# Two buffers for the tile of decays in the state-space part of a hybrid block, with decayed x and the states sharing one buffer and scaled x lying in the room of B

## The chip, the core and the metric

The kernel runs on one core of one Trainium2 chip. The metric is the device time of one launch in microseconds (us). The runs of the kernel before gave a median of 2721.82 us (2720.56, 2721.82 and 2723.49).

## What is computed

One layer of a residual block: an input projection of 512 tokens with 2048 channels, two branches (retention and a state-space scan, SSD), a projection of each back to 2048 channels, a gated merge and an output projection. The change touches the SSD scan alone. Cut to what matters (`xc` is x times its step size dt, `ac` the log decays of a chunk):

```python
def step(state, inp):
    xc, bc, cc, ac = inp
    acum = jnp.cumsum(ac, axis=1)
    seg = acum[:, :, None] - acum[:, None, :]
    decay = jnp.exp(jnp.where(causal, seg, -jnp.inf))
    cb = jnp.einsum('blgn,bsgn->blsg', cc, bc)
    y = jnp.einsum('blsg,blsgh,bsghp->blghp', cb, decay, xc)
    y = y + jnp.einsum('blgn,bghpn->blghp', cc, state) * jnp.exp(acum)[..., None]
    tail = jnp.exp(acum[:, -1:] - acum)
    state = (state * jnp.exp(acum[:, -1])[..., None, None]
             + jnp.einsum('bsgn,bsgh,bsghp->bghpn', bc, tail, xc))
    return state, y
```

There are 8 groups, each with its own B and C and with 8 heads of 64 channels; the kernel works in chunks of 128 tokens.

## The kernel before

All big projections go through `unit` (line 270). One unit multiplies 256 columns of a weight matrix with the normalized input, which stays in SBUF as a pair of fp32r tiles. Weights come in four loads (`wf`, line 244, on SP's queue); VectorE forms sums and differences of 128x128 blocks (lines 247, 252, 253), ScalarE rounds them to fp32r (`whi`, line 148), VectorE takes the remainder (`wlo`, line 149), and TensorE runs three matmuls of 256 columns for each of 7 blocks and 8 depths k (lines 230 to 232): 168 "block products" in a unit. `whi` has 7 buffers and `wlo` 6.

The SSD part (lines 593 to 709) lies between about 800 and 2010 us. For each group `g` one unit gives B and C; a convolution and SiLU (`conv`, lines 608 to 615) put them into `Bt` and `Ct`. `Bt` is transposed into `Bk` (lines 630 and 631), and `CB` is the masked product of `Bt` and `Ct` (lines 635 and 636); after line 635 nothing reads `Bt` until the next group writes it. Then, twice in a group (`jj`), a unit for x and a unit for z follow, and for each of the two halves `e` of the x unit a tile step:

- line 652 loads `E` on SP's queue; line 656 transposes x on TensorE; line 658 (VectorE) scales it into `xd`; line 661 (GpSimd, POOL) multiplies it by the decay to the end of its chunk into `xl`.
- line 665 (TensorE) forms the states from `xl` and `Bk`; lines 668 (ScalarE) and 672 (VectorE) carry them from chunk to chunk in `S`; line 693 (TensorE) multiplies them with `Ct`.
- line 678 loads `L`, two rows of cumulated log decays spread to 128 partitions, 512 KB, on SP's queue. Eight ScalarE instructions (line 682) and an exponential (line 684) make decays of it, VectorE multiplies by `CB` (line 685), and line 689 (TensorE) multiplies them with `xd`.
- lines 695 to 698 (VectorE) put the tile of y together, ScalarE squares and scales it, and it is stored.

So there are 32 tile steps: 8 groups, two pairs each, two halves in a pair. After each pair a gate unit is run (`gates`). `xd`, `xl`, `S`, `L` and `E` each have one buffer. Between the parts of a tile step stand block products of the next units, which the tile framework's scheduler sets there: it orders each engine's instructions by a model of their times and by priorities, and an engine then runs its instructions strictly in that order. Each of SP's loads waits in its queue for its buffer to come free, and what is queued behind it waits too.

The lines that the change touches are 657, 660, 667 and 677; in the changed kernel every line from 658 on has a number one higher.

Of the kernel before, what the change touches and what calls it, by code (L numbers as in the profile page):

```python
# [8 lines left out]
F32 = mybir.dt.float32  # L9
# [7 lines left out]
P = 128  # L17
T = 512
TB = T // P
# [108 lines left out]
def hybrid_block(tc, A, out):  # L128
# [15 lines left out]
    def att_tile():  # L144
        return att.tile([P, T], F32, name="att")
# [185 lines left out]
    def room(tag):  # L331
        return bg.tile([P, 8, 256], F32, name=tag, tag=tag)
# [170 lines left out]
    with tc.tile_pool(name="ret", bufs=1) as rp:  # L503
# [3 lines left out]
        for h in range(NH):  # L507
# [3 lines left out]
            c = h * DK  # L511
# [81 lines left out]
    with tc.tile_pool(name="ssd", bufs=1) as sp:  # L593

        cw = sp.tile([P, 48, 5], F32, name="cw")
        SP.dma_start(out=cw, in_=A["conv"])
        dsk = sp.tile([P, 32], F32, name="dsk")
        SP.dma_start(out=dsk, in_=A["dskip"])
        sq = R1
        sn = sp.tile([P, 32], F32, name="sn")  # L600
        SP.dma_start(out=sn, in_=A["ssd_norm_w"])
        g8 = room("A8").rearrange("p (n h) t -> p n (h t)", n=4)
        x8 = room("B8").rearrange("p (n h) t -> p n (h t)", n=4)
        Bt, Ct = g8[:, 0], g8[:, 1]
        Bk, CB = (g8[:, i].rearrange("p (c n) -> p c n", c=TB) for i in (2, 3))
        xs, sz = (x8[:, 0], x8[:, 1]), (x8[:, 2], x8[:, 3])

        def conv(x, j, dst):

            ACT.activation(dst, x, AF.Identity, scale=cw[:, j, 3:4], bias=cw[:, j, 4:5])  # L610
            for i in (2, 1, 0):
                s = 3 - i
                DVE.scalar_tensor_tensor(dst[:, s:], x[:, :T - s], cw[:, j, i:i + 1], dst[:, s:],
                                         op0=ALU.mult, op1=ALU.add)
            ACT.activation(dst, dst, AF.Silu)

        def gates(off, dst, i):
            w = w_in[:, off + i * 256:off + (i + 1) * 256]
            for e, x in enumerate(unit([w], plain=(2 * i + (off == GSO)) in PLAIN_M)):
                ACT.activation(x, x, AF.Sigmoid)  # L620
                ACT.dma_start(out=dst[(2 * i + e) * P:(2 * i + e + 1) * P, :], in_=x)

        todo = [(o, d, i) for i in range(NG) for o, d in ((GRO, gr_d), (GSO, gs_d))]
        for g in range(NG):
            xb, xc = unit([w_in[:, o + g * P:o + (g + 1) * P] for o in (BO, CO)], plain=g in PLAIN_B)
            conv(xb, 32 + g, Bt)
            conv(xc, 40 + g, Ct)
            ps = att_tile()
            for c in range(TB):
                PE.transpose(ps[:, c * P:(c + 1) * P], Bt[:, c * P:(c + 1) * P], ident)  # L630
            ACT.copy(Bk.rearrange("p c n -> p (c n)"), ps)
            ps = att_tile()
            for c in range(TB):
                sl = slice(c * P, (c + 1) * P)
                PE.matmul(ps[:, sl], Bt[:, sl], Ct[:, sl], start=True, stop=True)
            DVE.tensor_tensor(CB, ps.rearrange("p (c l) -> p c l", c=TB),
                              tri[:, None, :].to_broadcast([P, TB, P]), op=ALU.mult)

            for jj in range(2):
                j0 = g * 4 + jj * 2  # L640
                for e, x in enumerate(unit([w_in[:, XO + j0 * P:XO + (j0 + 2) * P]], plain=jj in PLAIN_X)):
                    conv(x, j0 + e, xs[e])
                for e, x in enumerate(unit([w_in[:, ZO + j0 * P:ZO + (j0 + 2) * P]], plain=jj in PLAIN_Z)):
                    ACT.activation(sz[e], x, AF.Silu)
                for e in range(2):
                    j = j0 + e
                    h0 = 2 * j
                    hs = slice(h0, h0 + 2)
                    y = xs[e]
                    E = sp.tile([P, T - P], F32, name="E")  # L650
                    for i in range(2):
                        SP.dma_start(out=E[i * 64:(i + 1) * 64, :], in_=E_d[h0 + i, P:].partition_broadcast(64))

                    ps = att_tile()
                    for c in range(TB):
                        PE.transpose(ps[:, c * P:(c + 1) * P], y[:, c * P:(c + 1) * P], ident)
                    xd = sp.tile([P, TB, 2, 64], F32, name="xd")
                    DVE.tensor_tensor(xd, ps.rearrange("p (c i d) -> p c i d", c=TB, i=2),  # L658
                                      dt[:, :, hs, None].to_broadcast([P, TB, 2, 64]), op=ALU.mult)
                    xl = sp.tile([P, TB - 1, 2, 64], F32, name="xl")  # L660
                    POOL.tensor_tensor(xl, xd[:, :TB - 1], tail[:, :TB - 1, hs, None].to_broadcast([P, TB - 1, 2, 64]),  # L661
                                       op=ALU.mult)
                    ps = att_tile()
                    for c in range(TB - 1):
                        PE.matmul(ps[:, c * P:(c + 1) * P], Bk[:, c, :], xl[:, c].rearrange("p i d -> p (i d)"),  # L665
                                  start=True, stop=True)
                    S = sp.tile([P, TB - 1, P], F32, name="S")
                    ACT.copy(S[:, 0, :], ps[:, :P])
                    for c in range(1, TB - 1):
                        for i in range(2):  # L670
                            d = slice(i * 64, (i + 1) * 64)
                            DVE.scalar_tensor_tensor(S[:, c, d], S[:, c - 1, d], cd[:, c, h0 + i:h0 + i + 1],
                                                     ps[:, c * P + i * 64:c * P + (i + 1) * 64],
                                                     op0=ALU.mult, op1=ALU.add)
                    pi = att_tile()

                    L = sp.tile([P, 2, TB, P], F32, name="L")
                    SP.dma_start(out=L.rearrange("p i c l -> p i (c l)"),
                                 in_=A_d[hs, :].partition_broadcast(P))
                    for i in range(2):  # L680
                        for c in range(TB):
                            ACT.activation(L[:, i, c, :], L[:, i, c, :], AF.Relu, scale=-1.0,  # L682
                                           bias=At[:, c, h0 + i:h0 + i + 1])
                    ACT.activation(L, L, AF.Exp, scale=-1.0)
                    DVE.tensor_tensor(L, L, CB[:, None].to_broadcast([P, 2, TB, P]), op=ALU.mult)

                    for c in range(TB):
                        for i in range(2):
                            PE.matmul(pi[i * 64:(i + 1) * 64, c * P:(c + 1) * P], xd[:, c, i, :], L[:, i, c, :],  # L689
                                      start=True, stop=True)  # L690
                    pe = att_tile()
                    for c in range(1, TB):
                        PE.matmul(pe[:, c * P:(c + 1) * P], S[:, c - 1, :], Ct[:, c * P:(c + 1) * P],  # L693
                                  start=True, stop=True)
                    DVE.scalar_tensor_tensor(y, y, dsk[:, j:j + 1], pi, op0=ALU.mult, op1=ALU.add)
                    DVE.tensor_tensor(E, pe[:, P:], E, op=ALU.mult)
                    DVE.tensor_tensor(y[:, P:], y[:, P:], E, op=ALU.add)
                    DVE.tensor_tensor(y, y, sz[e], op=ALU.mult)
                    if j == 0:
                        ACT.activation(sq, y, AF.Square)  # L700
                    else:
                        ACT.activation(sz[e], y, AF.Square)
                        POOL.tensor_tensor(sq, sq, sz[e], op=ALU.add)
                    ACT.activation(y, y, AF.Identity, scale=sn[:, j:j + 1])
                    ACT.dma_start(out=ys_d[j * P:(j + 1) * P, :], in_=y)
                if g or jj:
                    gates(*todo.pop(0))
        gates(*todo.pop(0))
# [3 lines left out]
    with tc.tile_pool(name="br", bufs=1) as bp:  # L712
        def rtile(src, j, t=None):
            if t is None:
                t = bp.tile([P, T], F32, name="f", tag="f", bufs=4)
            SP.dma_start(out=t, in_=src[j * P:(j + 1) * P, :])
            return t
# [22 lines left out]
        for i in range(NP):  # L740
# [4 lines left out]
            for e, x in enumerate(unit([w_s[D:, i * 256:(i + 1) * 256]], i % 2, i in PLAIN2)):  # L745
                j = 2 * i + e
                p = rtile(ps_d, j, last[:, e, :] if i == NP - 1 else None)
# [118 lines left out]
```

## Time and profile before

| | us |
|---|---|
| median of the runs | 2721.82 |
| profiled execution, whole | 2720.76 |
| its span, first to last instruction | 2719.0 |
| SSD part in it | 1210 (800 to 2010) |
| TensorE busy in the span | 2669.9 (98%) |
| VectorE busy | 2414.1 (89%) |
| ScalarE busy | 1346.0 (50%) |
| GpSimd busy | 186.3 (7%) |

The profile names TensorE's matmuls PE, its weight loads PEld, VectorE DVE, ScalarE ACT, GpSimd POOL and SyncE SP; "SPq" is SP's queue of issued loads. "L682" is line 682 of the kernel. A group's row gives line, engine, operation, tiles (written <- read) and count, then busy time and the mean duration of one in ns, then the idle time of the engine before it and what ended it. A row of the chain of waits gives start, length and what took that time. A row of the timeline gives start, length, engine, line, operation, tiles and count. A row of a table by stage gives a stretch, its length, and busy time and instructions of PE, PEld, DVE, ACT and POOL, the granted TensorE clock, the busy share of the DMA engines and GB/s. Weight names such as "pb" and "att" are PSUM tiles of the units and of the SSD's small products.

### The profile page before, as it was taken

How to read it: one execution, taken by the hardware profiler on the slowest of the kernel's cores; microseconds unless marked ns; L12 is line 12 of the kernel's file. 1: busy time of each engine (PE TensorE's matmuls, PEld its weight loads, DVE VectorE, ACT ScalarE, POOL GpSimd, SP SyncE). 2: the span in 40 equal slices, each digit the busy share in tenths (PEclk: the TensorE clock that was granted, in tenths of full speed). 3: DMA queues.
4: the chain of work that ended last, by engine and by line, in shares of the span. 5: the costliest groups of instructions: out<-in, count | busy, mean ns of one | idle time of the engine just before them, and what ended most of it. 6: DMA issues, size and time to landing. Idle time of an engine off the chain costs nothing.

```text
span 2719.0 us, 53156 instructions
## 1 busy us (share of the span) xinstructions
PE 2669.9 (98%) x21024; PEld 2579.4 (95%) x21024; DVE 2414.1 (89%) x3895; ACT 1346.0 (50%) x1906; POOL 186.3 (7%) x130
## 2 busy tenths in 40 slices
PE   7999999999999999999999999999999999999998
PEld 4899999999999999999999999999989989999897
DVE  7998888788878998999999998999989798799997
ACT  4434433343346656466665655555664354433543
POOL 0000000000000000000000001000000000011221
PEclk9999999999999999999999999999999999999999
DMA  4233333333333434344443434344454544557534
GB/s 159 86 96 109 95 105 105 99 101 105 105 99 115 131 119 134 117 130 123 138 135 126 138 108 134 114 137 132 137 196 151 192 156 147 179 179 237 197 124 140
DMA packets 339770, 362.54 MB, mean 133 GB/s; under 512 B 25152, under 2 KB 297792, under 8 KB 339520
## 3 DMA queue, kind: packets, MB, share of 16 engines
q1 hardware_dynamic: 319136, 325.05, 39.0%
q10 hardware_dynamic: 20384, 34.09, 3.4%
q8 instruction: 165, 2.70, 0.4%
q14 instruction: 85, 0.70, 0.1%
HBM read 321.56 MB, written 37.49 MB: 132 GB/s over the span
## 4 chain that ended last, share of the span: by engine, by line
PE 85%; DVE 6%; DMA 4%; issue 2%; ACT 2%; POOL 0%; SPq 0%; DVEq 0%; ACTq 0%; POOLq 0%
PE pb L230 23%; PE pb L232 23%; PE pb L231 23%; PE att L231 3%; PE att L232 3%; PE att L230 3%; DVE wlo L149 2%; PE att L572 1%; PE att L557 1%; PE att L689 1%; PE pb L118 1%; DMA L<-A_d 1%; PE att L665 1%; PE att L693 1%; PE att L118 1%
## 5 line engine op out<-in xcount | busy, mean ns | idle before, releaser
L148 ACT CAST whi<-wf 128x896 fp32r<-128x896 f32 (+1 forms) x968 | 833.3, 905 | 807.7 <-DVE wf L253 433.5
L149 DVE TENSOR_TENSOR wlo<-wf,whi 128x896 fp32r<-128x896 f32 (+1 forms) x968 | 1015.7, 1064 | 78.5 <-PE pb L232 48.6
L230 PE MATMUL pb<-a,whi 128*128 128x256 f32 (+1 forms) x3328 | 962.1, 294 | 6.4 <-ACT whi L148 2.6
L231 PE MATMUL pb<-a,whi 128*128 128x256 f32 (+1 forms) x3328 | 966.1, 293 | 0.0
L232 PE MATMUL pb<-a,wlo 128*128 128x256 f32 (+1 forms) x3328 | 954.2, 292 | 5.2 <-DVE wlo L149 5.2
L230 PEld LDWEIGHTS pb<-a,whi 128*128 128x128 f32 x3328 | 636.1, 192 | 19.7 <-ACT whi L148 3.8
L230 PE MATMUL pb<-b,whi 128*128 128x256 f32 x2304 | 654.3, 284 | 0.0
L231 PE MATMUL pb<-b,whi 128*128 128x256 f32 x2304 | 653.4, 284 | 0.0
L231 PEld LDWEIGHTS pb<-a,whi 128*128 128x128 f32 x3328 | 637.5, 192 | 11.8 <-issue 1.3
L232 PE MATMUL pb<-b,wlo 128*128 128x256 f32 x2304 | 648.2, 284 | 0.0
L232 PEld LDWEIGHTS pb<-a,wlo 128*128 128x128 f32 x3328 | 630.0, 192 | 18.7 <-DVE wlo L149 6.8
L231 PEld LDWEIGHTS pb<-b,whi 128*128 128x128 f32 x2304 | 442.3, 192 | 0.0
L230 PEld LDWEIGHTS pb<-b,whi 128*128 128x128 f32 x2304 | 442.1, 192 | 0.0
L232 PEld LDWEIGHTS pb<-b,wlo 128*128 128x128 f32 x2304 | 439.7, 192 | 0.2
L247 DVE TENSOR_TENSOR wf<-wf 128x512 f32<-128x512 f32 x432 | 303.5, 702 | 46.3 <-DMA wf<-in_w_in_dram 28.8
L253 DVE TENSOR_TENSOR wf<-wf 128x256 f32<-128x256 f32 x432 | 190.7, 441 | 1.7
L252 DVE TENSOR_TENSOR wf<-wf 128x256 f32<-128x256 f32 x432 | 186.8, 432 | 0.6
L231 PE MATMUL att<-a,whi 128*128 128x256 f32 (+1 forms) x480 | 145.7, 305 | 0.0
L230 PE MATMUL att<-a,whi 128*128 128x256 f32 (+1 forms) x480 | 145.5, 305 | 0.0
L232 PE MATMUL att<-a,wlo 128*128 128x256 f32 (+1 forms) x480 | 144.8, 306 | 0.7 <-DVE wlo L149 0.7
L682 ACT ACTIVATE L<-L,sst 128x128 f32<-128x128 f32 x256 | 78.7, 389 | 56.0 <-DMA L<-A_d 55.9
L661 POOL TENSOR_TENSOR xl<-xd,sst 128x384 f32<-128x384 f32 x32 | 46.3, 1446 | 809.7 <-DVE xd L658 809.7
(218 smaller groups left out, 2777.9 us busy)
## 6 DMA issues: line engine op xcount, KB each, us to landing
wf<-in_w_in_dram SPq DMA_DIRECT2D x640, 256.0 KB, 3.0
wf<-in_w_br_ssd_dram SPq DMA_DIRECT2D x128, 256.0 KB, 3.3
wf<-in_w_out_dram SPq DMA_DIRECT2D x72, 256.0 KB, 3.2
wf<-in_w_in_dram SPq DMA_DIRECT2D x128, 128.0 KB, 2.7
L<-A_d SPq DMA_DIRECT2D x32, 512.0 KB, 4.2
wf<-in_w_br_ret_dram SPq DMA_DIRECT2D x64, 256.0 KB, 3.5
ys_d<-B ACTq DMA_DIRECT2D x32, 256.0 KB, 2.1
r<-ys_d SPq DMA_DIRECT2D x16, 512.0 KB, 6.0
```

The costliest lines, as they stand in the source:

```text
L118: ins = getattr(self.engine, name)(*args, **kw).ins
L148: ACT.copy(dst_hi, src)
L149: return DVE.tensor_tensor(dst_lo, src, dst_hi.bitcast(F32), op=ALU.subtract).ins.name
L230: PE.matmul(o, wh, xh, start=b not in started, stop=False, skip_group_check=True)
L231: PE.matmul(o, wh, xl, start=False, stop=False, skip_group_check=True)
L232: PE.matmul(o, wl, xh, start=False, stop=(k == NP - 1), skip_group_check=True)
L247: first = DVE.tensor_tensor(f2[:, :, 4:6, :], f2[:, :, 1:3, :], f2[:, :, 0:1, :].to_broadcast([P, 2, 2, P]), op=ALU.subtract)
L252: DVE.tensor_tensor(f2[:, :, 0, :], f2[:, :, 2, :], f2[:, :, 4, :], op=ALU.add)
L253: DVE.tensor_tensor(f2[:, :, 6, :], f2[:, :, 3, :], f2[:, :, 0, :], op=ALU.subtract)
L557: PE.matmul(ps[:, :n], k[:, i, sb * P:(sb + 1) * P], q[:, i, sb * P:], start=(i == 0), stop=(i == 1))
L661: POOL.tensor_tensor(xl, xd[:, :TB - 1], tail[:, :TB - 1, hs, None].to_broadcast([P, TB - 1, 2, 64]), op=ALU.mult)
L682: ACT.activation(L[:, i, c, :], L[:, i, c, :], AF.Relu, scale=-1.0, bias=At[:, c, h0 + i:h0 + i + 1])
```

## The change

```diff
-                    xd = sp.tile([P, TB, 2, 64], F32, name="xd")
+
+                    xd = Bt.rearrange("p (c i d) -> p c i d", c=TB, i=2)
                     DVE.tensor_tensor(xd, ps.rearrange("p (c i d) -> p c i d", c=TB, i=2),
                                       dt[:, :, hs, None].to_broadcast([P, TB, 2, 64]), op=ALU.mult)
-                    xl = sp.tile([P, TB - 1, 2, 64], F32, name="xl")
+                    xl = sp.tile([P, TB - 1, 2, 64], F32, name="xl", tag="xl")
...
-                    S = sp.tile([P, TB - 1, P], F32, name="S")
+                    S = sp.tile([P, TB - 1, P], F32, name="S", tag="xl")
...
-                    L = sp.tile([P, 2, TB, P], F32, name="L")
+                    L = sp.tile([P, 2, TB, P], F32, name="L", bufs=2)
```

`xd` no longer has a tile of its own: it is written over `Bt`, which by then has been used. `xl` and `S` take turns in one buffer: `S` of a tile step lies where its `xl` lay, and the next `xl` where that `S` lay. `L` has two buffers. In bytes of a partition `L` takes 4096 more, `xd` 2048 and `S` 1536 fewer. No instruction is added or taken away in the arithmetic; the scheduler, which sees other buffers, orders the engines' work otherwise from the first group on.

ScalarE at the start of the SSD part, where B and C of the first group get their SiLU (line 615, tile A); before:

```order
L682 ACTIVATE L<-L,sst 128x128 x6
L148 CAST whi<-wf 128x896
L682 ACTIVATE L<-L,sst 128x128 x2
L684 ACT_TABLE_LOAD
L684 ACTIVATE L<-L 128x1024
L286 COPY o<-pb_8740 128x256
L615 ACT_TABLE_LOAD
L615 ACTIVATE A_8474<-A_8474 128x512 x2
L631 COPY A_8474<-att 128x512
L148 CAST whi<-wf 128x896 x4
```

And now, at the same place:

```order
L683 ACTIVATE L<-L,sst 128x128 x6
L148 CAST whi<-wf 128x896
L683 ACTIVATE L<-L,sst 128x128 x10
L685 ACT_TABLE_LOAD
L685 ACTIVATE L<-L 128x1024
L286 COPY o<-pb_8740 128x256
L615 ACT_TABLE_LOAD
L615 ACTIVATE A_8474<-A_8474 128x512
L685 ACT_TABLE_LOAD
L685 ACTIVATE L<-L 128x1024
L615 ACT_TABLE_LOAD
L615 ACTIVATE A_8474<-A_8474 128x512
```

The decays of the second tile step stand here too: eight more instructions of line 683 ahead of the SiLU of B, and an exponential with two table loads between the SiLU of B and that of C. On TensorE the transposes of B (line 630) stand 14 block products later than before, and 12 block products, not 14, stand between them and line 635.

SP's queue in the first group, from the first load of `L` on (the numbers behind names tell buffers of one name apart); before:

```order
L678 DMA L_9243<-A_d_89 128x1024
L244 DMA wf_9100<-in_w_in_dram 128x2x256 x2
L244 DMA wf_9135<-in_w_in_dram 128x2x256 x2
L244 DMA wf_9333<-in_w_in_dram 128x2x256 x2
L244 DMA wf_9389<-in_w_in_dram 128x2x256 x2
L244 DMA wf_9445<-in_w_in_dram 128x2x256 x2
L244 DMA wf_9480<-in_w_in_dram 128x2x256 x2
L678 DMA L_9297<-A_d_89 128x1024
L244 DMA wf_9577<-in_w_in_dram 128x2x256 x2
L244 DMA wf_9633<-in_w_in_dram 128x2x256 x2
L652 DMA E_9274<-E_d_90 64x384 x2
L678 DMA L_9832<-A_d_89 128x1024
```

And now:

```order
L679 DMA L_9242<-A_d_89 128x1024
L679 DMA L_9295<-A_d_89 128x1024
L244 DMA wf_9100<-in_w_in_dram 128x2x256 x2
L244 DMA wf_9135<-in_w_in_dram 128x2x256 x2
L244 DMA wf_9331<-in_w_in_dram 128x2x256 x2
L244 DMA wf_9387<-in_w_in_dram 128x2x256 x2
L244 DMA wf_9443<-in_w_in_dram 128x2x256 x2
L244 DMA wf_9478<-in_w_in_dram 128x2x256 x2
L679 DMA L_9829<-A_d_89 128x1024
L244 DMA wf_9575<-in_w_in_dram 128x2x256 x2
L679 DMA L_9883<-A_d_89 128x1024
L652 DMA E_9273<-E_d_90 64x384 x2
```

Each load of `L` stands one tile step earlier, and each still waits for a product of line 689 (now 690): that of two tile steps before, where it was that of the last one. The load of `E` for the second half of a pair stands behind such a load.

GpSimd in the first two pairs, with what each instruction waits for; before:

```order
L661 TENSOR_TENSOR xl<-xd,sst 128x384 [waits DVE_49]
L703 TENSOR_TENSOR R_81<-R_81,B_8475 128x512 [waits DMAHW1_49,Activation_49]
L661 TENSOR_TENSOR xl<-xd,sst 128x384 [waits DVE_49] x2
L703 TENSOR_TENSOR R_81<-R_81,B_8475 128x512 [waits Activation_49]
L703 TENSOR_TENSOR R_81<-R_81,B_8475 128x512 [waits Activation_49,Pool_49]
```

And now:

```order
L662 TENSOR_TENSOR xl<-A_8474,sst 128x384 [waits DVE_49,PE_49,Activation_49]
L704 TENSOR_TENSOR R_81<-R_81,B_8475 128x512 [waits DMAHW1_49,Activation_49]
L662 TENSOR_TENSOR xl<-A_8474,sst 128x384 [waits DVE_49,Pool_49]
L662 TENSOR_TENSOR xl<-A_8474,sst 128x384 [waits PE_49,Activation_49]
L704 TENSOR_TENSOR R_81<-R_81,B_8475 128x512 [waits Activation_49]
```

`xl` of the second half of a pair now waits for TensorE: for the last product of line 693 (now 694) of the first half, which reads `S`. On TensorE 28, 29 or 36 block products stand between that product and line 666, which reads the new `xl`.

The rest of the order: from the second group to the seventh it repeats itself now group by group (before, from the fourth on). Behind the SSD part the order of ACT, DVE, POOL and SP is as it was.

## The prediction

> **What bounds the kernel now.** I read the page first, then TensorE's waits in the SSD part, then a table by stage, and last the chain and the timelines at the places where TensorE stood.
>
> ```profile
> PE 2669.9 (98%) x21024; PEld 2579.4 (95%) x21024; DVE 2414.1 (89%) x3895; ACT 1346.0 (50%) x1906; POOL 186.3 (7%) x130
> L<-A_d SPq DMA_DIRECT2D x32, 512.0 KB, 4.2
> ```
>
> TensorE is busy for 98% of the span, so this change, which takes no work from TensorE, can win only what TensorE loses by waiting in the SSD part, and the matmuls run slowly after a wait. The table by stage (core 0; stretch, its length, busy time of PE, PEld, DVE, ACT and POOL) shows how little that is:
>
> ```profile
> 800.00:900.00 100.00, 94.98 (x777) 93.49 (x777) 88.24 (x139) 58.72 (x89) 4.43 (x3) 0.97 0.38 119
> 1000.00:1100.00 100.00, 97.99 (x829) 95.98 (x828) 87.99 (x142) 63.16 (x96) 8.69 (x6) 1.00 0.47 140
> 1408.00:1562.00 154.00, 154.00 (x1316) 152.81 (x1315) 142.70 (x227) 91.99 (x138) 12.32 (x8) 1.00 0.42 128
> 1562.00:1718.00 156.00, 154.63 (x1316) 152.97 (x1315) 142.53 (x229) 91.91 (x138) 15.18 (x8) 1.00 0.42 129
> 1872.00:2010.00 138.00, 137.00 (x1171) 135.53 (x1170) 125.90 (x201) 77.61 (x118) 10.07 (x7) 1.00 0.44 137
> ...
> sum 1210.00, PE 1200.54 PEld 1188.05 DVE 1112.34 ACT 719.04 POOL 94.08; mean PE 133.39 PEld 132.01 DVE 123.59 ACT 79.89 POOL 10.45
> ```
>
> Of 1210 us TensorE idles 9.5 (1210 less 1200.54): 5.0 in the first 100 us, 2.0 around 1050, 1.4 and 1.0 in two late stretches. A group that runs undisturbed takes 154 us for its 1316 instructions with TensorE idle for none of it. So the SSD part is a repeating pattern without a stall, with a few stalls where the pattern begins or slips. What TensorE waited for in it:
>
> ```profile
> PE pb L232 <- DVE wlo L149: 3.0, 3, 2.2
> PE att L630 <- ACT A L615: 2.6, 1, 2.6
> PE att L665 <- POOL xl L661: 1.4, 1, 1.4
> PE att L693 <- DVE S L672: 0.6, 1, 0.6
> PE att L689 <- DVE L L685: 0.4, 1, 0.4
> ...
> ACT L L682 <- DMA L<-A_d: 55.9, 28, 3.5
> DVE L L685 <- ACT L L684: 11.3, 12, 2.4
> ```
>
> The wait that a second `L` seems made for is ACT's for the load of `L`: 55.9 us in 28 waits. But TensorE waited for the product `L` itself only once, for 0.4 us. ACT's wait matters only where casts or remainders queued behind it come too late. There is one such place, near 875 us. The chain of waits there:
>
> ```profile
> 864.23 4.84 DMA L<-A_d
> 869.09 2.45 ACT L L682 x8
> 871.82 1.28 ACT L684
> 873.11 1.07 ACT L L684
> 876.97 1.01 DVE wlo L149
> 878.02 0.79 PE pb L232 x2
> 878.81 0.21 PE pb L230
> ```
>
> ACT stands for the load, makes decays, DVE stands for the decays, and a remainder `wlo` for TensorE is queued behind DVE's product.
>
> **The change part by part.** First the price of a stall. Matmuls right after it start 0.21 us apart (last row above), ordinary ones 0.12 (the starts of the first two rows here; timeline of TensorE):
>
> ```profile
> 874.39 0.28 PE L230 MATMUL pb<-b,whi 128*128 128x256 f32 x1
> 874.51 0.28 PE L231 MATMUL pb<-b,whi 128*128 128x256 f32 x1
> 875.51 0.28 PE L231 MATMUL pb<-a,whi 128*128 128x256 f32 x1
> 878.02 0.79 PE L232 MATMUL pb<-a,wlo 128*128 128x256 f32 x2 [2.23 <-DVE wlo L149]
> ```
>
> The stall before 878.02 is 2.5 us (878.02 less 875.51), about 2.4 over an ordinary step. The granted clock of the first 100 us is 0.97, so 3 us of TensorE time were lost to a halved clock there (0.03 x 100), after two stalls of over 2 us: about 1.5 us each. A stall of over 2 us thus costs itself and 1.5 us; the one near 875 costs 3.9, and I take 4.0.
>
> The Trainium skill (TensorE: Matmul & The Clock Gate, section "What's actually happening") says that the clock halves after at least one idle window of about 3.4 us; by that rule neither stall, being shorter, would have slowed what followed, and the term of 4.0 would be 2.4 and the sum +0.1 instead of -1.5. The trace does not agree: the rows show 0.21 us a step after 2.23 us of idle time.
>
> Start of the SSD part. The timeline of ACT there, and TensorE's next instruction:
>
> ```profile
> 817.18 0.69 ACT L682 ACTIVATE L<-L,sst 128x128 f32<-128x128 f32 x2
> 817.89 1.28 ACT L684 ACT_TABLE_LOAD   x1
> 819.18 1.06 ACT L684 ACTIVATE L<-L 128x1024 f32<-128x1024 f32 x1
> 820.52 1.28 ACT L615 ACT_TABLE_LOAD   x1
> 821.81 1.15 ACT L615 ACTIVATE A<-A 128x512 f32<-128x512 f32 x2
> 822.49 0.66 PE L630 MATMUL att<-cc,A 128*128 128x128 f32 x4 [2.63 <-ACT A L615]
> ```
>
> TensorE's 2.6 us wait for line 630 ends when the SiLU of B does. The change puts eight more instructions of line 682 ahead of it. Eight took 2.45 us (row at 869.09), so SiLU of B ends 2.45 later. TensorE has 14 block products more to do before line 630: 14 x 0.12 = 1.7. The wait grows by 0.8. Then SiLU of C comes later by a table load, an exponential and a table load: 1.28 + 1.06 + 1.28 = 3.6, and by its own 0.6: 4.2 after that of B. TensorE fills this with line 630 (0.66) and 12 block products at 0.21 (2.5): a second wait of 1.0. With a longer halved clock, up to 1 us, the start costs 1.8 to 2.8; I take +2.5. The casts that now follow later (some 5 us) are hidden by the block products of the first two depths, 24 of which are left behind line 635.
>
> The stall near 875. The decays that DVE waits for there are now those of a later tile step, and their load is issued after line 689 of the pair's second half, as before. From the end of that product: 4.2 for the load, 2.45, a square of 0.6, 1.28 and 1.07 for the decays, 0.7 to scale y, 0.9 for the next cast and 1.01 for its remainder: 12.2 us. TensorE has 117 block products of the current unit left then, 117 x 0.12 = 14.0, and three products of line 693 (0.2 each). Before it ran 90 products in 11.8 us (863.7 to 875.5) and then stood. So this stall goes, with 2.4 us in hand: -4.0. What is late next is ACT's wait for the load, which stays at about 2 us a tile step, since the scheduler still sets line 682 where it believes the load to land; nothing that TensorE needs soon is queued behind it.
>
> `xl` in the room of `S`. POOL's instruction for the second half now starts after the last product of line 693 and no longer right after `xd`. On POOL nothing but the sum of squares (line 703) is queued behind it; TensorE waits for it at line 665. The cover is 28 block products (8 pairs), 29 (2) or 36 (6): 28 x 0.12 = 3.4 us.
>
> ```profile
> L661 POOL TENSOR_TENSOR xl<-xd,sst x32: 833/1581/3685, 843.9 to 1997.3; 128x384 f32<-128x384 f32 x32
> 1677.11 2.95 POOL L661 TENSOR_TENSOR xl<-xd,sst 128x384 f32<-128x384 f32 x1 [32.24 <-DVE xd L658]
> 1689.24 3.69 POOL L661 TENSOR_TENSOR xl<-xd,sst 128x384 f32<-128x384 f32 x1 [9.18 <-DVE xd L658]
> 1691.01 1.22 DVE L685 TENSOR_TENSOR L<-L,A 128x1024 f32<-128x1024 f32 x1
> 1692.15 0.55 DVE L696 TENSOR_TENSOR E<-att,E 128x384 f32<-128x384 f32 x1
> 1692.98 0.49 PE L665 MATMUL att<-xl,A 128*128 128x128 f32 x2 [1.37 <-POOL xl L661]
> ```
>
> With 0.28 us for the last matmul to end (its row's length above) and some 0.2 for two signals (an estimate), `xl` may take 2.9 us. The median is 1.58: covered, 0. The bounds are 0 and, at the longest 3.69, +0.8 in each of 8 pairs, +6.4. I take 0, the value nearest to the median: only the two of one group (2.95 and 3.69) would not have fitted.
>
> `xd` in `Bt`, `S` in `xl`: 0. The next group's B is written after two to three hundred block products (over 24 us); `S` is written after the matmuls whose result it copies, so its new wait for them is no later. `E` of the second half now stands behind a load of `L` that waits for line 689 of its own tile step. No row shows that wait; `E` is smaller than `L`, whose load lands in 4.2, and is used after at least 40 block products (4.8). If issuing behind `L` takes more than the 0.6 between, DVE waits up to 1 us in some pairs; DVE is busy for 1112 of 1210 us and can make that up: 0, and at the worst +2.
>
> The late stalls (around 1050, 1691 and 2005). By the table they cost 2.0, 2.0 (156 less 154) and 1.0. They are slips of one pattern and will go, but the new order has its own: I set as much for new ones, 0, with -5 and +5 as bounds.
>
> Sum: 2.5 - 4.0 + 0 + 0 = -1.5 us. The profiled execution took 2720.76, 1.1 below the median of the runs; so 2719.3 for it and 2720.3 for a median: **2720.3 us**, no change. About 0.2%, or 5.4 us, is what a measurement of this kernel can tell from none.
>
> **Rivals.**
>
> 1. `xl` becomes TensorE's wait in every group (slower). POOL was held up exactly while DVE ran instructions on two SBUF tiles, and ended in the first one that reads PSUM (line 696 in the rows above). `xl` now starts when two remainders `wlo` stand on DVE, and the pattern repeats seven times, so a hold-up would too. It decides from 2.9 us on: at 3.7 it is 8 x 0.8 = 6.4, and more if DVE's product with `CB` lies in it again (1.2): 8 x 1.2 = 9.6. With the start at +2.5 and the other terms at 0, 2721.8 + 2.5 + 6.4 = 2730.7. Against it: only one group of eight showed it. The Trainium skill (GPSIMD Engine Reference, section "Specifications") says that GpSimd shares its SBUF interfaces with VectorE and contends with instructions with two SBUF inputs; by that rule this rival is a mechanism and no accident, and the trace agrees with it by the 3.69 us.
>
> 2. All late stalls go and none comes (faster): 2720.3 - 5 = 2715.3, and with the halved clock after them and a start at its lower bound 2713. For it: an undisturbed group idles for none of its 154 us, and the new order takes on its repeated pattern two groups earlier. Against it: the order is still made by a model, and its loads still land later than it believes.
>
> 3. The second buffer does nothing that TensorE can feel (no change): the load is issued after a product as before, DVE's wait near 875 stays in some form, and only the start is dearer: 2721.8 + 2.5 = 2724.3.
>
> **How the numbers follow.** The forecast has 0.40, rival 3 0.12, rival 1 0.20, rival 2 0.23; 0.05 is left for casts that come late behind ACT's decays (slower). So faster 0.23, same 0.52, slower 0.25. The range reaches down to just below rival 2's lower value and up to rival 1's first: 2712 to 2731. The forecast's own range is 2715 to 2726.
>
> **What would show it.** Right: line 630's wait grows to over 3 us and a wait for line 635 of about 1 appears; no stall near 875; ACT's wait for `L` still tens of us; undisturbed groups of 154 us. Wrong: line 665 waits for `xl` in every group, or groups longer than 155 us, or TensorE's idle time in the SSD part under 5 us.

## The result, and the profile of the changed kernel

The changed kernel is slower: 2725.64 us (median of 20 runs) against 2721.52 (20 runs of the kernel before beside them), a ratio of 1.0017, 95% interval 1.0010 to 1.0024. The forecast was 2720.3 and no change. The loss of 4.1 us is smaller than the 0.2% that the prediction took as its limit, but 20 runs each tell it from nothing. The profiled execution took 2726.3 us, its span 2724.3.

TensorE does the same work in a longer span. The busy row of the changed kernel's page:

```profile
PE 2669.1 (98%) x21024; PEld 2579.3 (95%) x21024; DVE 2420.8 (89%) x3895; ACT 1337.7 (49%) x1905; POOL 182.3 (7%) x130
```

What TensorE waited for between 800 and 2020 us, and ACT's wait for the load of `L`:

```profile
PE pb L230 <- DVE o L289: 7.4, 8, 1.7
PE att L635 <- ACT A L615: 2.2, 1, 2.2
PE att L694 <- ACT S L669: 1.6, 1, 1.6
PE att L630 <- ACT A L615: 1.0, 1, 1.0
PE pb L230 <- DVE o L287: 0.7, 2, 0.3
PE pb L230 <- ACT o L286: 0.3, 1, 0.3
...
ACT L L683 <- DMA L<-A_d: 40.9, 13, 5.2
```

None of the old waits is left except that for line 630: none for `wlo`, none for `xl`. In their place stands a wait of a kind that before had for 0.3 us only, and for another line (287): TensorE stands eight times until VectorE has run line 289, the third of VectorE's four instructions that read a finished unit's PSUM tiles out into `o`. Line 289 frees the third tile, `pb2`, for the next unit.

One such wait lies in every group. The table by stage of the changed kernel (columns as before), cut at the ends of these waits:

```profile
1176.73:1332.12 155.39, 154.47 (x1317) 153.13 (x1317) 144.89 (x228) 90.99 (x140) 11.98 (x8) 1.00 0.42 128
```

A group takes 155.4 us, where an undisturbed one took 154.0. The wait at 1176, in the timelines of VectorE, of GpSimd and of TensorE:

```profile
1173.34 0.68 DVE L288 TENSOR_TENSOR o<-o,pb 128x512 f32<-128x512 f32 x1
1173.94 1.52 DVE L247 TENSOR_TENSOR wf<-wf 128x512 f32<-128x512 f32 x1
1175.38 0.41 DVE L253 TENSOR_TENSOR wf<-wf 128x256 f32<-128x256 f32 x1
1175.71 0.55 DVE L697 TENSOR_TENSOR E<-att,E 128x384 f32<-128x384 f32 x1
1176.18 0.41 DVE L289 TENSOR_TENSOR o<-o,pb 128x256 f32<-128x256 f32 x1
```

```profile
1173.61 1.29 POOL L704 TENSOR_TENSOR R<-R,B 128x512 f32<-128x512 f32 x1 [12.05 <-ACT B L703]
```

```profile
1175.72 0.28 PE L232 MATMUL pb<-b,wlo 128*128 128x256 f32 x1
1176.73 0.36 PE L230 MATMUL pb<-a,whi 128*128 128x256 f32 x1 [0.73 <-DVE o L289]
1176.93 0.28 PE L231 MATMUL pb<-a,whi 128*128 128x256 f32 x1
```

Between line 288 and line 289 VectorE runs three instructions for others, and the first of them, line 247, takes 1.52 us instead of 0.70 while GpSimd adds up squares (line 704). That the two meet comes with the new order: of the 213 runs of line 247 in the SSD part 19 take over 0.9 us beside such an addition now, and one did before, with the same 31 additions. The unit whose tiles are read out here is the gate unit after a group's first pair, and the one that waits is the x unit of the second pair: in the new order it comes to its third PSUM tile after 36 block products of its own, while in the regular groups of before it did so after 54. That is what makes line 289 urgent.

To see where the 4 us are, I took the time at which TensorE had done the same number of block products in both traces, the changed kernel less before, by before's clock:

| up to | difference, us | what lies in the step |
|---|---|---|
| 819 | +1.5 | code that is the same in both: a wait near 206, 1.78 us against 1.14, and slow matmuls behind it (+2.1, after -0.6 up to there) |
| 831 | +2.9 | start of the SSD part: +1.4 |
| 869 | +4.7 | wait for `S` before line 694, at 863.8: +1.8 |
| 881 | +1.1 | the stall near 875 is gone: -3.6 |
| 888 | +4.1 | first wait for line 289, at 882: +3.0 |
| 2012, and to 2372 | +4.8 | late groups: old stalls gone near 1050, 1691 and 2005 (-2.6, -2.0, -1.4), new ones +6.7: +0.7 |

So the SSD part makes 3.3 of the 4.8 us by which these two executions differ there. Near 882 (the z unit of the first group's second pair, which comes to its third tile after 36 block products in both orders) the wait is longer, GpSimd has no part in it (line 247 takes 0.69 us there), and the matmuls behind it are slow:

```profile
882.14 0.28 PE L232 MATMUL pb<-b,wlo 128*128 128x256 f32 x1
884.13 0.36 PE L230 MATMUL pb<-a,whi 128*128 128x256 f32 x1 [1.71 <-DVE o L289]
...
884.71 0.41 PE L230 MATMUL pb<-b,whi 128*128 128x256 f32 x1
884.93 0.41 PE L231 MATMUL pb<-b,whi 128*128 128x256 f32 x1
```

### The profile page after: what moved, and what is told of

The parts are those of the page before. It is cut to its first block, busy times and chain, and to the rows that moved or that the text cites. A ratio compares the mean times of both kernels' runs of the same rounds, so it can differ in the third digit from the quotient of the medians.

```text
span 2724.3 us, 53130 instructions
## 1 busy us (share of the span) xinstructions
PE 2669.1 (98%) x21024; PEld 2579.3 (95%) x21024; DVE 2420.8 (89%) x3895; ACT 1337.7 (49%) x1905; POOL 182.3 (7%) x130
## 4 chain that ended last, share of the span: by engine, by line
PE 82%; DVE 9%; DMA 4%; issue 3%; ACT 2%; SPq 0%; POOL 0%; DVEq 0%; ACTq 0%; POOLq 0%
PE pb L230 22%; PE pb L231 22%; PE pb L232 22%; DVE wlo L149 3%; PE att L232 2%; PE att L231 2%; PE att L230 2%; PE att L572 1%; PE att L557 1%; DVE wf L247 1%; PE att L690 1%; PE pb L118 1%; DMA mm_d<-f 1%; DMA wf<-in_w_br_ssd_dram 1%; PE att L118 1%
## 5 line engine op out<-in xcount | busy, mean ns | idle before, releaser
L247 DVE TENSOR_TENSOR wf<-wf 128x512 f32<-128x512 f32 x432 | 317.8, 736 | 46.9 <-DMA wf<-in_w_in_dram 24.2
L683 ACT ACTIVATE L<-L,sst 128x128 f32<-128x128 f32 x256 | 79.2, 390 | 60.9 <-DMA L<-A_d 40.9
L232 PEld LDWEIGHTS att<-a,wlo 128*128 128x128 f32 x480 | 90.9, 191 | 6.5 <-DVE wlo L149 2.8
```

What stands on the lines that cost most here:

```text
L232: PE.matmul(o, wl, xh, start=False, stop=(k == NP - 1), skip_group_check=True)
L247: first = DVE.tensor_tensor(f2[:, :, 4:6, :], f2[:, :, 1:3, :], f2[:, :, 0:1, :].to_broadcast([P, 2, 2, P]), op=ALU.subtract)
```

## The experiments

The first theory (O) was that the order costs the time, not the buffers. Its rivals: sharing rooms costs (R), the second buffer costs (D), GpSimd holds VectorE (H). Some kernels fix the order by hand: a list of each engine's instructions, taken from the order of another kernel, chained by dependencies that set order and no wait:

```diff
+        for e, z in FORCE.items():
+            ...
+            for a, b in zip(way, way[1:]):
+                tc.add_manual_dep(
+                    mine[b], mine[a].name,
+                    mybir.DependencyInfo(mybir.DependencyClass.NoSync, mybir.DependencyReason.DATA),
+                    reason="order of issue")
```

The list stands ahead of the code, so line numbers in their profiles are 10 higher. Ratios are against the kernel before on the same chip.

| | ratio to before | 95% interval |
|---|---|---|
| the change | 1.0017 | 1.0010 to 1.0024 |
| e1, `xd` in `Bt` alone | 1.0002 | 0.9994 to 1.0011 |
| e2, both rooms, one `L` | 1.0012 | 1.0004 to 1.0021 |
| e3, the change in before's order | 1.0003 | 0.9992 to 1.0013 |
| e4, the change, line 289 early | 0.9993 | 0.9984 to 1.0001 |
| e5, the change, start reordered | 0.9995 | 0.9984 to 1.0005 |
| e6, e4 and e5 together | 0.9969 | 0.9959 to 0.9979 |
| e7, e6 and an early copy of `S` | 0.9966 | 0.9954 to 0.9979 |
| e8, the change without line 704 | 0.9995 | 0.9984 to 1.0006 |
| e9, before with its start reordered | 0.9994 | 0.9986 to 1.0003 |

**e1.** One part of the change alone:

```diff
-                    xd = sp.tile([P, TB, 2, 64], F32, name="xd")
+                    xd = Bt.rearrange("p (c i d) -> p c i d", c=TB, i=2)
```

> The kernel before with one part of the change: xd lies in Bt, and nothing else. Every engine's instructions stand in the order of before. Theory O (the loss of about 4 us lies in the new order of the instructions: a dearer start of the SSD part, +4.7, a stall of about 1 us in each group before TensorE's third PSUM tile, +8, and old stalls gone, -8): no change, within 2 us of before, with the old stalls near 875, 1050, 1691 and 2005 in their places. Rival R (sharing rooms costs time whatever the order): slower by 2 us or more, with waits for xd or Bt that before does not show.

It keeps the order of before on every engine, and the time: the waits are those of before to 0.3 us each. `xd` in `Bt` costs nothing that can be told.

**e2.** The changed kernel with `name="L"` in place of `name="L", bufs=2`.

> Both shared rooms, xd in Bt and xl with S, but one buffer for L. The scheduler makes an order of its own from it (neither that of before nor that of the change). Theory O: the start as before (line 630 the one wait, 2.6 us), the stall near 875 still there, and what the late groups do is a matter of this order: a total within 4 us of before either way, and any difference sits in named stalls behind a late instruction, none of them for xl. Rival R: about +4 us like the whole change, with waits for xl or S. Rival D (the second buffer of L is itself what costs): the time of before within 2 us.

TensorE's waits in the SSD part:

```profile
PE pb L232 <- DVE wlo L149: 3.1, 4, 1.4
PE att L630 <- ACT A L615: 2.7, 1, 2.7
...
PE att L666 <- POOL xl L662: 1.6, 2, 1.0
PE att L694 <- DVE S L673: 1.6, 1, 1.6
```

It is 3 us slower (0.0012 x 2719). The start and the stall near 875 are as O had them, but two waits for `xl` are there, against O, and R had about this loss. This run doesn't part the two; it shows that the rooms alone already change the order and the time, and D's "within 2 us" is missed by a little.

**e3.** The buffers of the change, the order of before; one matmul of line 694 moved ahead by five places.

> All buffers of the changed kernel, L twice and both shared rooms, but every engine's instructions forced into the order of before (one matmul of line 694 in the second group moved ahead by five places, since it must read S before xl is written over it). Theory O: the time of before within 2 us, 4 us under the change; the start with the one wait for line 630, no stall of 1 us in each group, the old late stalls back; near 875 perhaps less, since the load of L is no longer late, though ACT's place for it is the old one. Rival R and rival D: still slower than before by about 4 us, since buffers, loads and waits are those of the change.

The time of before, as O had it; but the interval, 0.9992 to 1.0013, still touches that of the change. The waits tell more than that:

```profile
PE att L676 <- POOL xl L672: 5.3, 6, 1.9
PE att L640 <- ACT A L625: 2.6, 1, 2.6
PE pb L242 <- DVE wlo L159: 2.0, 2, 1.2
PE pb L240 <- ACT whi L158: 1.3, 2, 0.8
```

The waits for lines 635 and 289 that the change has are absent or small (0.5 us for line 289, here 299). Not all late stalls came back (those near 1691 and 2005 but for 0.6 us are gone, that near 875 is split into three), but TensorE now waits six times for `xl` (line 666, here 676), where before waited once, for 1.4 us. In the order of before too little work stands between line 694 and line 666, mostly 11 or 15 block products where the change has 28 to 36, to hide that `xl` waits for the room of `S`. So R's mechanism is real, some 4 us more, in an order made without the shared room; the order of the change covers it, and has no wait for `xl`. It is not what makes the change slow. That the time came out as that of before is in part luck: waits of 12.2 us in all stand here against 9.3, with others in them.

**e4.** The changed kernel in its own order, with line 289 right behind line 288 in all units of the SSD part. VectorE at the place shown above:

```diff
 L288 TENSOR_TENSOR o<-o,pb 128x512
+L289 TENSOR_TENSOR o<-o,pb 128x256
 L247 TENSOR_TENSOR wf<-wf 128x512
 L253 TENSOR_TENSOR wf<-wf 128x256
 L697 TENSOR_TENSOR E<-att,E 128x384
-L289 TENSOR_TENSOR o<-o,pb 128x256
```

> The changed kernel with one kind of instruction moved: in every unit of the SSD part VectorE runs line 289 right behind line 288 (it stood 1 to 6 instructions later), so that TensorE's third PSUM tile comes free some 0.4 to 3 us earlier. Theory O: the repeated stalls of 0.8 to 1.1 us (948, 1020, 1176, 1331, 1486, 1642, 1797, 1952) and that of 1.9 near 882 go; groups of 154.2 us instead of 155.4; 6 to 10 us under the change, so 2 to 6 under before. Rival H (the stall is VectorE being held by GpSimd's sum of squares, and goes wherever VectorE's next instruction is): the stall stays in part, groups over 155 us, less than 3 us won. Rivals R and D: no change against the changed kernel.

0.24% under the change by the two ratios (1.0017 less 0.9993), 6.5 us. The table by stage, with TensorE busy for the whole of a group again:

```profile
1168.40:1322.60 154.20, 154.20 (x1318) 153.03 (x1317) 144.91 (x228) 90.97 (x139) 13.15 (x8) 1.00 0.42 129
```

The wait for line 289 shrank from 7.4 us in eight to 0.3 in one. VectorE's line 247 still runs beside GpSimd's sum, one place behind 289, and delays nobody. R and D had no change here: the loss can be taken away, and more than it, with every buffer left as it is. H's first form (the hold hits whatever comes next) falls too.

**e5.** ScalarE at the start; the exponential and its eight instructions are those of the second tile step:

```diff
 L683 ACTIVATE L<-L,sst 128x128 x2
-L683 ACTIVATE L<-L,sst 128x128 x8
 L685 ACTIVATE L<-L 128x1024
 L286 COPY o<-pb 128x256
 L615 ACTIVATE A<-A 128x512
-L685 ACTIVATE L<-L 128x1024
 L615 ACTIVATE A<-A 128x512
...
 L610 ACTIVATE B<-o,cw 128x512 x2
+L683 ACTIVATE L<-L,sst 128x128 x8
+L685 ACTIVATE L<-L 128x1024
```

On VectorE the product of line 686 for that step stands ahead of the first line 696.

> The changed kernel with its start alone reordered: ScalarE makes the decays of the second tile step (eight of line 683 and an exponential) behind the first two of line 610 for x, where it stood idle for 5.8 us, and no longer ahead of the SiLU of B and C; VectorE's product of line 686 for that step stands ahead of its first line 696. Theory O: the waits for lines 630 and 635 (1.1 and 2.4 us) and the half-speed matmuls behind them (about 2 us) go, the SiLU of both standing 5 us earlier; the stalls in each group stay; 4 to 6 us under the change, so 0 to 2 under before. Rival C (the start's loss is not these waits but the casts and loads that come late with them, and moves elsewhere): less than 2 us under the change, with a stall between 835 and 865 in place of those.

0.22% under the change, 6.0 us: as O had it in size. Both waits of the start are gone, and with them the slow matmuls; the waits for line 289 stayed (6.5 us in eight). O's figure of +4.7 for the start was too high, though: by the count of block products above the change itself lost 1.4 there against before. The edit wins more than that because before pays for its start too (the 2.6 us wait for line 630), and the transposes of line 630 now have 14 block products more ahead of them.

**e6.** Both edits.

> The changed kernel with both reorderings: line 289 right behind line 288 on VectorE, and the decays of the second tile step behind line 610 on ScalarE. Theory O: the two losses have different places and add up: 10 to 13 us under the change, 6 to 9 under before, 2 to 6 under either reordering alone. Rival C: about the time of line 289's reordering alone.

They add up: 0.48% under the change, 13 us, and 0.31% (8.4 us) under before, by an interval that leaves no doubt. The timeline of ScalarE at the start, and TensorE's waits in the whole SSD part:

```profile
819.69 1.15 ACT L625 ACTIVATE A<-A 128x512 f32<-128x512 f32 x2
...
824.57 1.52 ACT L620 ACTIVATE B<-o,cw 128x512 f32<-128x512 f32 x2
826.00 2.44 ACT L693 ACTIVATE L<-L,sst 128x128 f32<-128x128 f32 x8
```

```profile
PE att L676 <- POOL xl L672: 1.1, 1, 1.1
PE pb L242 <- DVE wlo L159: 0.5, 1, 0.5
PE pb L240 <- DVE o L300: 0.4, 1, 0.4
PE pb L240 <- DVE o L297: 0.3, 1, 0.3
PE pb L240 <- DVE o L299: 0.3, 1, 0.3
```

2.6 us of waits in all, where before had 9.3 and the change 13.2.

**e7.** e6 with one instruction of ScalarE moved:

```diff
+L669 COPY S<-att 128x128
 L644 ACTIVATE B<-o 128x512 x2
-L669 COPY S<-att 128x128
```

> As the run with both reorderings, and ScalarE copies the second tile step's first states (line 669) ahead of the SiLU of z (line 644) and its table load, not behind: TensorE's wait for S at line 694 near 861 (1.1 to 1.7 us) goes. Theory O: 1 to 2 us under the run with both. If that wait has another cause: no change.

No difference that can be told (0.9966 and 0.9969). The wait that it was to take away had gone in e6 already, with the earlier start; the expectation had overlooked that. It is among the two fastest versions, and no more can be said.

**e8.** The changed kernel less line 704. Its norm uses the squares of the first tile alone. The order of the other four engines is that of the change.

```diff
-                        POOL.tensor_tensor(sq, sq, sz[e], op=ALU.add)
```

> The changed kernel without GpSimd's sum of squares (line 704), so that the norm uses the squares of the first tile alone; the order of TensorE, VectorE, ScalarE and SyncE is that of the change to the instruction. Rival H (VectorE's line 247 is held by it, 1.52 instead of 0.70 us, and that is the stall): line 247 takes 0.70 each time, and the stall of each group shrinks by the 0.8 us of that, from 1.0 to 0.2 or nothing; 5 to 7 us under the change. Theory O in its plain form (the order alone, line 289 is too late by itself): the stall stays over 0.5 us, and less than 3 us are won.

H's numbers, not those of O in its plain form: 0.22% (6.0 us) under the change, and the waits of the groups are gone (two are left, 1.7 of 1.9 us near 882). VectorE at the place shown for the change:

```profile
1169.35 0.67 DVE L288 TENSOR_TENSOR o<-o,pb 128x512 f32<-128x512 f32 x1
1169.95 0.68 DVE L247 TENSOR_TENSOR wf<-wf 128x512 f32<-128x512 f32 x1
...
1171.36 0.40 DVE L289 TENSOR_TENSOR o<-o,pb 128x256 f32<-128x256 f32 x1
```

From the start of line 288 to the end of line 289 it takes 2.41 us here and 3.25 in the change (1173.34 to 1176.59); the 0.84 between them is what line 247 lost (1.52 less 0.68). So the theory had to be mended: the new order leaves line 289 nothing in hand, and GpSimd's hold of 0.8 us then falls on TensorE. Either taken away, order (e4) or hold (e8), ends it in seven of the eight groups. The longer wait near 882 has no hold in it; e4 ends it and e8 does not.

**e9.** The kernel before, its order and buffers, with its first tile step's decays (lines 682 and 684) behind line 610, and the first line 685 ahead of the first line 658.

> The kernel before, its own buffers and its own order, with the same kind of edit at the start: the decays of the first tile step (eight of line 682 and an exponential) stand behind the first two of line 610 for x, and VectorE's product of line 685 for that step ahead of its first line 658. It asks what is left of the second buffer of L once the start is equally good in both. Theory O: the wait for line 630 (2.6 us) and the half speed behind it (some 2) go, 4 to 5 us under before; the stalls near 875, 1016 to 1084, 1691 and 2005 stay, and with them 3 to 5 us over the changed kernel with both reorderings. Rival E (the buffers are worth nothing, and a good start is all): the time of the changed kernel with both reorderings, 8 us under before.

Both missed in part. The wait for line 630 went, and by the count of block products before's start became 4.4 us earlier (from +0.9 to -3.5), as O had it. But 1.9 were given back near 880 and all but 1.1 by 2012: the stalls that follow grew, so the run is only 0.06% (1.6 us, where O had 4 to 5) under before, with an interval that takes in no change. Its waits:

```profile
PE pb L242 <- DVE wlo L159: 3.7, 4, 2.2
PE pb L240 <- ACT whi L158: 2.2, 3, 0.9
PE att L675 <- POOL xl L671: 1.4, 1, 1.4
```

E falls as well: with an equally freed start the two buffers of `L` and their order (e6) stand 0.25% under e9, some 7 us. Which of the two, buffers or order, holds that difference was not tried, and neither was before's order with its late stalls freed by hand as well.

## Why the prediction was wrong, point by point

- **Start, +2.5.** +1.4 by the count of block products; the sign and the cause were right, the two waits were not. Line 630's was to grow to over 3 us and shrank to 1.0. The eight instructions did cost ScalarE 2.3 us, but by TensorE's count it had come to line 610, ahead of them, 1.7 us earlier (at 811.24 against 811.48, with 1.5 between the counts), which the prediction had not looked for; so the SiLU of B was 0.6 us late and not 2.45. Line 635's wait was to be 1.0 and was 2.2. The SiLU of C did come 4.3 us after that of B, for which 4.2 was reckoned; but the 12 block products between them were reckoned at 0.21 us, and after the wait of 0.96 us they came 0.12 apart:

```profile
824.60 0.66 PE L630 MATMUL att<-cc,A 128*128 128x128 f32 x4 [0.96 <-ACT A L615]
...
826.28 0.28 PE L231 MATMUL pb<-b,whi 128*128 128x256 f32 x1
826.40 0.28 PE L232 MATMUL pb<-b,wlo 128*128 128x256 f32 x1
828.91 1.35 PE L635 MATMUL att<-A 128*128 128x128 f32 x8 [2.23 <-ACT A L615]
```

- **The stall near 875, -4.0.** It went, for -3.6. What failed is the step behind it: "What is late next is ACT's wait for the load", with "nothing that TensorE needs soon" queued behind it. First, the copy of `S` (line 669) was queued there. The chain that ends TensorE's wait at 863.8 goes back to a load of `L`:

```profile
851.98 4.42 DMA L<-A_d
856.48 2.46 ACT L L683 x8
...
861.22 1.77 ACT whi L148 x2
863.00 1.28 ACT L644
...
864.84 0.61 ACT B L644
865.45 0.15 ACT S L669
```

ScalarE stood 3.5 us for this load, then made the decays, two casts, a table load and the SiLU of z one after another, and copied `S` behind them; TensorE stood for it 1.6 us, +1.8 in the table. Second came the wait for line 289 at 882 (+3.0). The prediction had followed the queues of SP and ScalarE past the stall, and not VectorE's, where the instructions stand that free TensorE's PSUM tiles. The old stall had hidden this wait: in before TensorE, held up near 875, came to the same product at 881.48, and line 289 had ended at 881.33. The two, +4.8, are more than the whole +3.3 of the SSD part. Without them the sum would have been -1.5, the prediction's own only by luck: +1.4, -3.6 and +0.7, where it had +2.5, -4.0 and 0. Of the +3.0 some 1.5 is half speed behind the wait, which the same wait in e8 did not bring (last section).

- **`xl` in the room of `S`, 0.** Right for this order: no wait for `xl` in the change. e3 shows what rival 1 saw: in the order of before the room does cost, 5.3 us in six waits, 3.9 more than before has. That is under rival 1's 6.4, and in another order than the one that it spoke of. Its reading that GpSimd's hold-up ended in line 696 does not come out of the rows either: they end at 1692.93 and at 1692.70.
- **`xd` in `Bt`, `S` in `xl`, `E`: 0.** Right for `xd` (e1); no wait for `E` or for `S` on account of the room is among TensorE's.
- **Late stalls, 0.** Right in sum (+0.7: -6.0 and +6.7), wrong in kind. The text set "as much for new ones" without naming one, and that the two nearly cancel is luck; what came was one wait repeated in each group. Groups longer than 155 us were named as a sign that the forecast is wrong, and they are what the trace shows.
- **ACT's wait for the load** stayed in tens of us, as said (40.9, from 55.9). At least one of its waits reached TensorE, by the copy of `S`, as shown above.
- **Rival 3** gave the nearest time, 2724.3, by another way: it had the stall near 875 stay in some form and no other gain, while in fact the old stalls did go, 9.6 us of them, and new ones of 11.5 took their places.

## What to carry to other kernels

When a stall goes, ask what the waiting engine needs next, on every queue: here a copy behind ScalarE's decays, and the instructions that read PSUM out, which stand among other work on a vector engine that is busy for 93% of the time (144.9 of 155.4 us). A second buffer changes more than the wait it is made for where a scheduler sets the order: read the new order at each place that frees something for the bounding engine, and if the loss is there, try to move those instructions before giving the buffer up; here two moves made of a loss of 0.17% a gain of 0.31%. That the gain needs the second buffer is not shown.

## What the runs showed of the hardware

- VectorE and GpSimd hold each other. The prediction reckoned with GpSimd being held; the other way round cost more: line 247, which reads two parts of an SBUF tile, took 1.52 us instead of 0.68 beside a GpSimd addition of 1.29 us, and 1.07 in e4 at another offset. It looks as if VectorE stood until GpSimd was done: in all 19 such runs of the change line 247 ended 0.55 us after the addition, whenever it had started (1175.46 against 1174.90 in the rows at 1173). Its mean over the SSD part was 0.77 us in the change and 0.69 without the additions. The Trainium skill (GPSIMD Engine Reference, section "Specifications") has the two contend where an instruction of VectorE has two SBUF inputs, as this one has; the trace agrees, by the 0.84 us.
- TensorE's speed after a wait: idle for 0.96 us, and the next block products still came 0.12 us apart; idle for 1.71 us (row at 884.13), and they came 0.21 apart until 887.7. Behind the 2.2 us wait for line 635 half speed lasted until 833.1. The length of the wait does not settle it, though. The same wait as at 884.13 in e8's trace, 1.70 us, was followed by full speed, and so were one of 1.88 us in e2 (at 208.88) and one of 1.94 in e3 (at 914.26), while every wait of over 2 us in the SSD part was followed by some half speed. What decides between 1.7 and 2 us no run here shows. e8:

```profile
883.73 0.36 PE L230 MATMUL pb<-a,whi 128*128 128x256 f32 x1 [1.70 <-DVE o L289]
883.92 0.28 PE L231 MATMUL pb<-a,whi 128*128 128x256 f32 x1
884.04 0.28 PE L232 MATMUL pb<-a,wlo 128*128 128x256 f32 x1
```

- A stretch of code that is the same in both kernels can differ by 1.5 us between two executions (the wait near 206 us), a third of the effect measured here. That is why single steps are read from counts within one stretch and the verdicts from medians.
